# Layer 0 attention: the last 24 modulation columns as TensorE products between the query tiles

## The chip, the cores and the metric

The kernel runs on one core of one Trainium2 chip. Its time is the device time of one execution in microseconds. Three executions of the kernel before took 2327.45, 2328.95 and 2331.25 us, so the median is 2328.95 us. The profile is of one further execution.

The names of the engines here are those of the profile: PE is the matrix engine (TensorE), PEld its weight loads, DVE the vector engine, ACT the scalar engine, POOL GpSimd, and SP the engine that issues most DMAs.

## The reference, cut to what matters

The model has two layers. Layer 0 modulates its normed tokens with shifts, scales and gates that come from a conditioning vector, once for the latent tokens (condition `c`) and once for the context tokens (condition `c_ctx`):

```python
def adaln(cond, w, b):
    return jax.nn.silu(cond) @ w + b

mod_lat = adaln(c, mod_w[i], mod_b[i])[:, None, :]
mod_ctx = adaln(c_ctx, mod_w[i], mod_b[i])[None, None, :]
sh1, sc1, g1, sh2, sc2, g2 = jnp.split(mod_lat, N_MOD, axis=-1)
csh1, csc1, cg1, csh2, csc2, cg2 = jnp.split(mod_ctx, N_MOD, axis=-1)
```

`mod_w[0]` is 1024 x 6144. Cut into blocks of 128 outputs it has 48 blocks, called columns in the kernel, since each gives one column of 128 numbers per condition. Blocks 0 to 15 are `sh1` and `sc1`, 16 to 23 the gate `g1` behind the attention, 24 to 39 `sh2` and `sc2` of the feed-forward, 40 to 47 the gate `g2`. This case is about blocks 16 to 39, both conditions: 24 blocks, 48 results.

The attention of layer 0 has 6 heads. Each has two score matrices, and the second softmax is subtracted from the first, scaled by lambda. There are 512 latent queries with 768 keys, and 256 context queries with 256 keys.

## The kernel before, in words

Products with weights are made in three passes (`mm3`): weights and activations are split into a high and a low part (fp32r), and PE multiplies high by high, high by low and low by high, at lines L108, L109 and L110. A product of plain f32 operands is shown as two PE records for each instruction.

In the attention the work goes by units: a head h (0 to 5) and a query tile u (0 to 5) of 128 queries. For each unit `scores` (L428) makes the two score matrices of the next tile in the PSUM tile `pS`; DVE takes the row maximum (L407) and ACT the exponential (L408). Then `combine` works on the present tile: DVE joins the two softmax matrices (L447), PE transposes the result in blocks of 128 into `ptr` (L452), ACT and DVE split that into high and low (L133), and at every second tile PE multiplies by the values into `prb` (L108 to L110 with `prb`), which ACT copies out (L461). There is one buffer `prb`. Between these parts a generator `fill` gives out the input projection of the next head (L108 to L110 with `pz`), and in heads 0 and 1 the pooling branch.

The columns are fitted in one a unit, from unit 1 on (24 units, so to the first of head 4), by `mod_both`. For each column SP loads a 128 x 1024 block of the transposed weight (L288). DVE multiplies it by the row of condition 0 and sums along the row in one instruction (L292). POOL then multiplies the block by the row of condition 1 in four pieces of 256 (L301), and ACT sums it (L303). The bias is added later for all columns at once (`mod_bias`, L307).

The order on each engine is made by a scheduler that walks the program with its own estimates of times; the program's order and the `behind` hints bound it. Each engine runs its queue strictly in that order, so an instruction that waits holds up all that stand behind it on the same engine. Input weights are loaded into three buffers `w_raw` (L87), which SP issues in one queue with the column loads.

Of the kernel before, what the change touches and what calls it, by code (L numbers as in the profile page):

```python
# [43 lines left out]
def behind(tc, ins):  # L44

    return tc.issue_after(getattr(ins, "ins", ins))
# [16 lines left out]
class Kernel:  # L63
# [228 lines left out]
            nc.vector.scalar_tensor_tensor(self.m_junk, w, 1.0, self.crow[:, cd, :], op0=OP.mult, op1=OP.mult,  # L292
                                           accum_out=self.mods[:, layer, cd, n:n + 1])

    def mod_both(self, n):


        self.mod_dve(0, n, (0,))
        w = self.m_raw[(self.m_next - 1) % len(self.m_raw)]
        for i in range(0, D, 256):  # L300
            self.nc.gpsimd.tensor_mul(w[:, i:i + 256], w[:, i:i + 256], self.crow[:, 1, i:i + 256])  # L301
        yield
        self.nc.scalar.activation(w, w, AF.Copy, accum_out=self.mods[:, 0, 1, n:n + 1])  # L303

    def mod_bias(self, layer, t0, n, cd):
        m = self.mods[:, layer, cd, t0:t0 + n]
# [127 lines left out]
    def combine(self, h, u, sc):  # L434


        nc, wk, wb, sm = self.nc, self.work, self.workb, self.small
        (p0, p1), z, nkt = sc
        if u == 0:
            self.oT = wb.tile([128, TA], F32, name="oT", bufs=2)  # L440
        if u % 2 == 0:
            self.pt = [wb.tile([128, 6, 256], F32R, name=f"pt{x}", bufs=1) for x in "hl"]
        (pth, ptl), oT = self.pt, self.oT
        rz = sm.tile([128, 1], F32, name="rz", bufs=4)
        nc.vector.reciprocal(rz, z[:, 1, u:u + 1])
        nc.vector.tensor_scalar(rz, rz, z[:, 0, u:u + 1], self.nlam, op0=OP.mult, op1=OP.mult)
        ins = nc.vector.scalar_tensor_tensor(p0, p1, rz, p0, op0=OP.mult, op1=OP.add)  # L447
        for k0 in range(0, nkt, 4):
            n = min(4, nkt - k0)
            pt = self.ps.tile([128, 4, 128], F32, name="ptr", bufs=1)  # L450
            for k in range(n):
                nc.tensor.transpose(pt[:, k, :], p0[:, (k0 + k) * 128:(k0 + k + 1) * 128], self.ident)  # L452
            qs = slice(u % 2 * 128, u % 2 * 128 + 128)
            self.split(pth[:, k0:k0 + n, qs], ptl[:, k0:k0 + n, qs], pt[:, :n])
        if u % 2:
            vh, vl = self.heads[h][2]
            kt0 = 6 - nkt
            po = self.ps.tile([128, 512], F32, name="prb", bufs=1)[:, :256]
            self.mm3(po, lambda i: (vh[:, kt0 + i, :], vl[:, kt0 + i, :]),
                     lambda i: (pth[:, i, :], ptl[:, i, :]), n=nkt)  # L460
            nc.scalar.copy(oT[:, u // 2 * 256:u // 2 * 256 + 256], po)  # L461

        if u < 2:
            next(self.head_end, None)
        if u == 5:
            self.head_end = self.norm_head(h, oT, z)
            next(self.head_end)
            if h == 5:
                for _ in self.head_end:
                    pass  # L470
        return ins
# [76 lines left out]
    def layer0_mixer(self):  # L548
        nc, I, tc = self.nc, self.I, self.tc
        self.mix_d = self.dram.tile([KT - 2, 128, TA], F32, name="mix_d")  # L550
        with ExitStack() as ctx:
            a = self.a = self.new_a(LAT, CTX)
            mspace = self.hm.tile([128, KT * TA], F32, name="hm")
            self.m_space = self.mod_space(mspace, 2)
            wk = self.work = self.pool(ctx, "workA")
            c2 = ctx.enter_context(ExitStack())
            xp = self.xp = self.pool(c2, "xp")
# [41 lines left out]
            with behind(tc, self.m_after):  # L599
                nc.sync.dma_start(self.pw, I["pool_w"])  # L600
                nc.sync.dma_start(lmb, I["lam"][None, :, :].to_broadcast([128, 4, 64]))
                self.cond_rows()
            norm(blat, LAT)

            def lam():
# [24 lines left out]
                pass  # L630
            c2 = ctx.enter_context(ExitStack())
            self.workb = self.pool(c2, "workB")
            self.m_raw.append(self.workb.tile([128, D], F32, name="m3", bufs=1))
            self.head_end = iter(())
            todo, sums = list(range(16, 40)), iter(())
            fill = {0: [self.inproj_head(1), self.pool_branch(0)], 1: [self.inproj_head(2), self.pool_branch(1)],
                    2: [self.inproj_head(3)], 3: [self.inproj_head(4)], 4: [self.inproj_head(5)],
                    5: [self.out_latent()]}
# [2 lines left out]
            for i, (h, u) in enumerate(units):  # L641
# [8 lines left out]
                            next(g, None)  # L650
                if u == 5 and h < 5:
                    nxt, pe = self.scores(h + 1, 0)
                with behind(tc, self.exped):
                    next(sums, None)
                if todo and i:
                    with behind(tc, dv):
                        sums = self.mod_both(todo.pop(0))
                        next(sums)
                cur = nxt
            c2.close()  # L660
            for _ in fill[5][0]:
# [8 lines left out]
    def out_latent(self):  # L670

        nc, I, wk, tc = self.nc, self.I, self.work, self.tc
        for cd in range(2):
            self.mod_bias(0, 16, 8, cd)
        self.mix = self.new_a(LAT, CTX)
        for k in range(KT - 1):
            if k == KT - 2:
# [21 lines left out]
    def out_rest(self):  # L699
# [12 lines left out]
        for d in range(KT - 3, KT):  # L712
# [3 lines left out]
                for e in range(KT - 3):  # L716
                    last(e, 0)
            full(d, 0)
        for cd in range(2):
            self.mod_bias(0, 24, 16, cd)  # L720
        self.hm_d = self.dram.tile([128, KT, TA], F32, name="hm_d")
        self.B = {}
        hi, lo = (self.big.tile([128, KT, TL], F32R, name=f"a{x}512").rearrange("p k t -> p (k t)") for x in "hl")
# [1075 lines left out]
def tiles(w, nt=128):  # L1799

    K, N = w.shape
    return np.ascontiguousarray(w.reshape(K // 128, 128, N // nt, nt).transpose(2, 1, 0, 3)).reshape(N // nt, 128, -1)
# [35 lines left out]
def layouts(inp):  # L1838
# [8 lines left out]
    A["gains"] = cols(np.stack([a["norm1_g"][0], a["norm2_g"][0], a["norm1_g"][1], a["norm2_g"][1]]))  # L1847
    A["misc"] = np.concatenate([cols(a["pool_scale"][0]), cols(a["q_norm_g"][0]), cols(a["kv_norm_g"][0])], axis=1)
    A["mod_n"] = tiles(a["mod_w"][0][:, :2048], 512)
    A["mod_t"] = np.ascontiguousarray(a["mod_w"].transpose(0, 2, 1)).reshape(2, 48, 128, D)  # L1850
    w = a["even_w_in"][0]
    order = [w[:, :256]]
# [67 lines left out]
```

## Time and profile before

| what | value |
|---|---|
| median of three runs | 2328.95 us |
| profiled execution, its own time | 2319.6 us |
| its span, first to last instruction | 2317.9 us |
| PE busy over the span | 2251.2 us, 97% |
| DVE busy | 1765.4 us, 76% |
| ACT busy | 1212.2 us, 52% |
| POOL busy | 198.3 us, 9% |
| mean granted clock of PE | 0.989 |

Busy time is the union of an engine's records. PE's records overlap, as one matmul starts before the last has drained, so the time that one really takes is read from start to start. The attention of layer 0 runs from about 85 to 415 us of the span. A granted clock of 1.00 is 2.4 GHz, of 0.50 it is 1.2 GHz.

### The profile page before, as it was taken

What the parts mean: (1) busy time and instruction counts of PE and PEld (TensorE: products, weight loads), DVE (VectorE), ACT (ScalarE), POOL (GpSimd) and SP (SyncE); (2) the same over time, 40 slices, a digit from 0 to 9 for tenths busy, and PEclk for the clock granted to TensorE, in tenths of its full rate; (3) what the DMA queues carried; (4) which work ended last, traced back from release to release, by engine and by line L of the source; (5) the groups of instructions that cost most, each with busy time, mean ns of one, the idle gap of its engine ahead of it and who ended that gap; (6) DMA issues with size and microseconds to landing.
All of it is one profiled execution on the core that took longest, in us unless ns stands there. A gap on an engine that the chain in (4) does not pass through costs nothing.

```text
span 2317.9 us, 31085 instructions
## 1 busy us (share of the span) xinstructions
PE 2251.2 (97%) x11672; PEld 1833.2 (79%) x11672; DVE 1765.4 (76%) x2547; ACT 1212.2 (52%) x1690; POOL 198.3 (9%) x273
## 2 busy tenths in 40 slices
PE   8999998999999999999999899999999999999996
PEld 3777777899999988888888777777777777777774
DVE  4779876687877876477775798787877778777897
ACT  3445553453334432245553676566655666555764
POOL 0033410000000111000000000010000000000030
PEclk9999998999999999999999999999999999999998
DMA  7233322335444596311122797787777877777794
GB/s 295 80 105 106 107 77 95 110 132 165 143 141 152 198 377 240 126 42 42 35 85 78 275 362 293 282 304 274 266 276 275 315 263 288 267 285 272 275 399 175
DMA packets 97505, 467.97 MB, mean 202 GB/s; under 512 B 11232, under 2 KB 13664, under 8 KB 63556
## 3 DMA queue, kind: packets, MB, share of 16 engines
q1 hardware_dynamic: 76000, 386.83, 45.9%
q0 software_dynamic: 19680, 76.90, 9.2%
q10 hardware_dynamic: 1668, 2.18, 0.3%
q8 instruction: 94, 1.54, 0.3%
q14 instruction: 63, 0.52, 0.1%
HBM read 435.19 MB, written 30.68 MB: 201 GB/s over the span
## 4 chain that ended last, share of the span: by engine, by line
PE 85%; DVE 6%; ACT 2%; DMA 1%; issue 1%; POOL 0%; DVEq 0%; ACTq 0%
PE pz L109 11%; PE pz L108 11%; PE pz L110 11%; PE pS L818 10%; PE pS L973 5%; PE pz L818 4%; PE pS L108 4%; PE pS L109 4%; PE pS L110 3%; PE pz L1490 3%; PE pz L1489 3%; PE pz L973 2%; PE prb L108 1%; PE prb L109 1%; PE prb L110 1%; DVE u_lo L133 1%
## 5 line engine op out<-in xcount | busy, mean ns | idle before, releaser
L133 DVE TENSOR_TENSOR u_lo<-u_raw,u_hi 128x2048 fp32r<-128x2048 f32 x264 | 601.8, 2285 | 154.7 <-ACT u_hi L133 154.5
L133 ACT CAST u_hi<-u_raw 128x2048 fp32r<-128x2048 f32 x264 | 502.4, 1909 | 199.5 <-issue 69.6
L109 PE MATMUL pz<-u_lo,x 128*128 128x512 f32 x704 | 283.7, 403 | 6.2 <-DVE u_lo L133 6.0
L108 PE MATMUL pz<-u_hi,x 128*128 128x512 f32 x704 | 282.0, 401 | 0.5 <-ACT u_hi L133 0.5
L110 PE MATMUL pz<-u_hi,x 128*128 128x512 f32 x704 | 279.9, 398 | 0.0
L108 PE MATMUL pz<-ah,w_hi 128*128 128x512 f32 (+1 forms) x513 | 183.4, 358 | 1.1 <-DVE n_tmp L325 0.6
L109 PE MATMUL pz<-al,w_hi 128*128 128x512 f32 (+1 forms) x513 | 178.8, 349 | 0.0
L110 PE MATMUL pz<-ah,w_lo 128*128 128x512 f32 (+1 forms) x513 | 178.2, 348 | 0.0
L109 PEld LDWEIGHTS pz<-u_lo,x 128*128 128x128 f32 x704 | 132.5, 188 | 46.0 <-DVE u_lo L133 18.7
L108 PEld LDWEIGHTS pz<-u_hi,x 128*128 128x128 f32 x704 | 132.4, 188 | 29.9 <-ACT u_hi L133 1.0
L110 PEld LDWEIGHTS pz<-u_hi,x 128*128 128x128 f32 x704 | 132.5, 188 | 28.5
L292 DVE SCALAR_TENSOR_TENSOR n_acc<-ms 128x1024 bf16<-128x1024 f32 x80 | 97.4, 1217 | 19.0 <-DMA ms<-in_mod_t_dram 18.9
L108 PEld LDWEIGHTS pz<-ah,w_hi 128*128 128x128 f32 x513 | 97.3, 190 | 14.9 <-issue 0.9
L97 ACT CAST w_hi<-w_raw 128x1024 fp32r<-128x1024 f32 (+2 forms) x69 | 58.6, 851 | 93.3 <-PE pz L109 63.2
L110 PEld LDWEIGHTS pz<-ah,w_lo 128*128 128x128 f32 x513 | 97.2, 190 | 11.0 <-issue 0.5
L109 PEld LDWEIGHTS pz<-al,w_hi 128*128 128x128 f32 x513 | 97.6, 190 | 10.5 <-issue 0.7
L109 PE MATMUL pS<-u_lo,hs 128*128 128x512 f32 x264 | 105.1, 398 | 0.7 <-DVE u_lo L133 0.7
L1489 PE MATMUL pz<-u_hi,x 128*128 128x512 f32 x264 | 105.3, 399 | 0.0
L108 PE MATMUL pS<-u_hi,hs 128*128 128x512 f32 x264 | 104.6, 396 | 0.5 <-ACT hs L133 0.5
L110 PE MATMUL pS<-u_hi,hs 128*128 128x512 f32 x264 | 104.6, 396 | 0.0
L1490 PE MATMUL pz<-u_lo,x 128*64 128x512 f32 x264 | 98.5, 394 | 0.0
L408 ACT ACTIVATE P<-pS,mx 128x768 f32<-128x768 f32 (+1 forms) x104 | 83.3, 804 | 19.7 <-DVE mx L407 19.4
(561 smaller groups left out, 5431.8 us busy)
## 6 DMA issues: line engine op xcount, KB each, us to landing
u_raw<-in_moe_w_dram SPq DMA_DIRECT2D x264, 1024.0 KB, 4.9
ms<-in_mod_t_dram POOLq DMA_DIRECT2D x56, 512.0 KB, 4.9
hr<-hid_d SPq DMA_DIRECT2D x38, 384.0 KB, 6.0
w_raw<-in_w_gate_dram SPq DMA_DIRECT2D x28, 512.0 KB, 3.5
w_raw<-in_w_in_dram SPq DMA_DIRECT2D x27, 512.0 KB, 3.3
u<-in_w_up_dram SPq DMA_DIRECT2D x22, 512.0 KB, 3.7
w_raw<-in_w_dn_dram SPq DMA_DIRECT2D x22, 512.0 KB, 4.7
hid_d<-hm POOLq DMA_DIRECT2D x22, 384.0 KB, 3.1
```

What stands on the lines that cost most here:

```text
L97: nc.scalar.copy(hi[:, :n], raw[:, :n])
L108: nc.tensor.matmul(ps, wh, xh, start=first and i == 0, stop=False)
L109: nc.tensor.matmul(ps, wh, xl, start=False, stop=False)
L110: ins = nc.tensor.matmul(ps, wl, xh, start=False, stop=last and i == n - 1)
L133: return nc.scalar.copy(hi, src), nc.vector.tensor_sub(lo, src, hi)
L292: nc.vector.scalar_tensor_tensor(self.m_junk, w, 1.0, self.crow[:, cd, :], op0=OP.mult, op1=OP.mult, accum_out=self.mods[:, layer, cd, n:n ...
L408: self.exped = nc.scalar.activation(P, S, AF.Exp, bias=nm, accum_out=z)
L818: nc.tensor.matmul(ps, w[m][:, c], x[n][:, k, :], start=first and k == i == 0, stop=k == 3 and i == 2, skip_group_check=True)
L973: nc.tensor.matmul((pl, px)[cd][d], W[w][:, d * 128:d * 128 + 128], x[v][:, s], start=n == i == 0 and not (cd and d % 2), stop=n == NF - 1 ...
L1489: m = [lambda s, e: self.nc.tensor.matmul(ps, x[2][:, k, :], w(k)[0], start=s, stop=e), lambda s, e: self.nc.tensor.matmul(ps[:64], x[0][: ...
L1490: lambda s, e: self.nc.tensor.matmul(ps[:64], x[0][:, k, :], w(k)[1], start=s, stop=e)]
```

## The change

The 24 columns leave DVE, POOL and ACT and become products on PE. The weight block itself, in its plain layout (`mod_k`, 128 inputs x 128 outputs for each of 8 slices), is the stationary operand, and the two conditions' silu vectors `scol` are two moving columns. One column takes 8 matmuls into two PSUM columns. Two columns (16 matmuls) are done at every second tile, u = 1, 3 and 5, from head 0 to head 3, 12 times in all, ahead of the tile's transposes. The PSUM tile is the one that the product with the values uses later in the same tile (`prb`, its columns 256 to 259); it is taken at the start of `combine` for that. A small DVE addition adds the bias and stores both columns. There are four weight buffers, all loaded ahead by SP, and each is loaded again after its use. The rows of the conditions (`cond_rows`) are no longer loaded here, and the two late additions of the bias are gone.

```diff
-    def mod_both(self, n):
-        self.mod_dve(0, n, (0,))
-        w = self.m_raw[(self.m_next - 1) % len(self.m_raw)]
-        for i in range(0, D, 256):
-            self.nc.gpsimd.tensor_mul(w[:, i:i + 256], w[:, i:i + 256], self.crow[:, 1, i:i + 256])
-        yield
-        self.nc.scalar.activation(w, w, AF.Copy, accum_out=self.mods[:, 0, 1, n:n + 1])
+    def mod_load(self):
+        if self.m_next < 24:
+            self.nc.sync.dma_start(self.m_raw[self.m_next % len(self.m_raw)], self.I["mod_k"][self.m_next])
+            self.m_next += 1
+
+    def mod_cols(self, ps, i0):
+        nc = self.nc
+        for i in range(2):
+            w = self.m_raw[(i0 + i) % len(self.m_raw)]
+            for k in range(KT):
+                nc.tensor.matmul(ps[:, 2 * i:2 * i + 2], w[:, k * 128:k * 128 + 128], self.scol[:, k, :], start=k == 0,
+                                 stop=k == KT - 1, skip_group_check=True)
+            self.mod_load()
+        n = slice(16 + i0, 18 + i0)
+        nc.vector.tensor_add(self.mods[:, 0, :, n], ps.rearrange("p (n c) -> p c n", c=2),
+                             self.modb[:, 0, None, n].to_broadcast([128, 2, 2]))
...
         (p0, p1), z, nkt = sc
+        if u % 2:
+            po = self.ps.tile([128, 512], F32, name="prb", bufs=1)
+            if self.m_todo:
+                self.mod_cols(po[:, 256:260], self.m_todo.pop(0))
+            po = po[:, :256]
...
             kt0 = 6 - nkt
-            po = self.ps.tile([128, 512], F32, name="prb", bufs=1)[:, :256]
             self.mm3(po, lambda i: (vh[:, kt0 + i, :], vl[:, kt0 + i, :]),
...
-                self.cond_rows()
+                for _ in self.m_raw:
+                    self.mod_load()
...
-                with behind(tc, self.exped):
-                    next(sums, None)
-                if todo and i:
-                    with behind(tc, dv):
-                        sums = self.mod_both(todo.pop(0))
-                        next(sums)
                 cur = nxt
...
-        for cd in range(2):
-            self.mod_bias(0, 16, 8, cd)
...
-        for cd in range(2):
-            self.mod_bias(0, 24, 16, cd)
...
+    A["mod_k"] = tiles(a["mod_w"][0][:, 2048:5120])
```

What the scheduler makes of it is seen in the order on the engines. First PE, in head 0 at tile 1, before the change: `pS` are the scores of the next tile, `ptr<-ident,P` the transposes of this one, and `pz` the input projection of head 1.

```order
L428 MATMUL pS<-qk1h,qk0h 128x256 x2
L428 MATMUL pS<-qk1l,qk0h 128x256 x2
L428 MATMUL pS<-qk1h,qk0l 128x256 x2
L452 MATMUL ptr<-ident,P_627 128x128 x4
L108 MATMUL pz<-ah_98,w_hi 128x256
```

The same place in the changed kernel, with line numbers moved (L437 is L428 of before, L466 is L452):

```order
L437 MATMUL pS<-qk1h,qk0h 128x256 x2
L437 MATMUL pS<-qk1l,qk0h 128x256 x2
L437 MATMUL pS<-qk1h,qk0l 128x256 x2
L307 MATMUL prb<-scol,hm 128x2 x16
L466 MATMUL ptr<-ident,P_628 128x128 x4
L108 MATMUL pz<-ah_98,w_hi 128x256
```

One row is new: 16 matmuls of two columns, between the scores of the next tile and the transposes of this one. There are 12 such rows on PE, one for each pair of columns.

The second place is ACT in head 0 at tiles 2 to 4, before the change: `hm,mods<-hm` is the sum of a column (L303), which reads what POOL has multiplied; `w_hi` is the split of the next weights, and `sq` belongs to the pooling branch.

```order
L133 CAST pth<-ptr 128x4x128
L408 ACTIVATE P_874,zs<-pS,mx 128x768
L408 ACTIVATE P_875,zs<-pS,mx 128x768
L303 ACTIVATE hm,mods<-hm 128x1024
L133 CAST pth<-ptr 128x2x128
L408 ACTIVATE P_964,zs<-pS,mx 128x256
L408 ACTIVATE P_965,zs<-pS,mx 128x256
L303 ACTIVATE hm,mods<-hm 128x1024
L133 CAST qk1h<-pz 128x256
L97 CAST w_hi<-w_raw 128x1024
```

The same place on ACT in the changed kernel (L417 is L408 of before, L543 is L530):

```order
L133 CAST pth<-ptr 128x4x128
L417 ACTIVATE P_887,zs<-pS,mx 128x768
L417 ACTIVATE P_888,zs<-pS,mx 128x768
L133 CAST pth<-ptr 128x2x128
L417 ACTIVATE P_970,zs<-pS,mx 128x256
L417 ACTIVATE P_971,zs<-pS,mx 128x256
L97 CAST w_hi<-w_raw 128x1024
L133 CAST qk1h<-pz 128x256
```

Both sums are gone from ACT's queue, and the casts that stood behind them follow the exponentials at once.

## Rows read from the trace of the kernel before

**Rows 1.** The page, part 1: busy time, share of the span, instructions.
```profile
PE 2251.2 (97%) x11672; PEld 1833.2 (79%) x11672; DVE 1765.4 (76%) x2547; ACT 1212.2 (52%) x1690; POOL 198.3 (9%) x273
```

**Rows 2.** Busy us by stretch: PE, PEld, DVE, ACT, POOL; PEclk, DMA share, GB/s.
```profile
100.00:120.00 20.00, 19.56 (x126) 15.52 (x124) 19.75 (x35) 9.67 (x22) 5.13 (x10) 1.00 0.16 54
120.00:140.00 20.00, 17.74 (x110) 14.23 (x112) 14.57 (x31) 10.31 (x22) 11.59 (x15) 1.00 0.36 125
140.00:160.00 20.00, 19.27 (x108) 14.59 (x107) 17.78 (x33) 10.18 (x21) 7.11 (x9) 1.00 0.38 124
160.00:200.00 40.00, 36.12 (x221) 28.46 (x219) 33.17 (x57) 19.11 (x42) 10.71 (x14) 1.00 0.26 87
200.00:250.00 50.00, 48.68 (x313) 39.07 (x311) 43.80 (x87) 29.64 (x66) 24.56 (x29) 1.00 0.33 114
250.00:300.00 50.00, 49.29 (x311) 39.20 (x309) 42.09 (x83) 28.30 (x62) 19.09 (x25) 1.00 0.30 103
300.00:350.00 50.00, 49.35 (x315) 39.64 (x314) 37.67 (x81) 27.92 (x61) 5.54 (x9) 1.00 0.20 68
350.00:400.00 50.00, 44.16 (x230) 34.37 (x230) 30.42 (x67) 19.00 (x45) 3.19 (x6) 0.86 0.28 100
```

**Rows 3.** The chain that ended last, 85 to 350 us, shares by line.
```profile
by line: PE pz L108 11.9%; PE pz L110 11.6%; PE pz L109 11.6%; PE pS L428 6.8%; PE ptr L452 4.8%; DVE w_lo L98 3.3%; issue 3.0%; PE prb L108 3.0%; DVE n_acc L292 2.8%; PE prb L169 2.8%; PE prb L109 2.5%; DVE mx L407 2.4%; PE prb L110 2.1%; 
```

**Rows 4.** Lines L292, L301 and L303: ns min/median/max, first and last start, form.
```profile
L292 DVE SCALAR_TENSOR_TENSOR n_acc<-hm x16: 1206/1218/1760, 93.0 to 294.6; 128x1024 bf16<-128x1024 f32 x16
...
L301 POOL TENSOR_TENSOR hm<-hm x64: 722/737/1723, 94.3 to 298.0; 128x256 f32<-128x256 f32 x64
...
L303 ACT ACTIVATE hm<-hm x16: 1047/1055/1066, 112.5 to 312.7; 128x1024 f32<-128x1024 f32 x16
```

**Rows 5.** PE in order of time, 136.9 to 139 us: start, us, engine, line, operation.
```profile
137.07 0.28 PE L110 MATMUL pz<-ah,w_lo 128*128 128x256 f32 x1
137.38 1.50 PE L169 MATMUL prb<-ones,sq 128*128 128x1 f32 x12
138.74 0.36 PE L108 MATMUL pz<-ah,w_hi 128*128 128x256 f32 x1
138.94 0.28 PE L109 MATMUL pz<-al,w_hi 128*128 128x256 f32 x1
```

**Rows 6.** PE in order of time, 1264.9 to 1268.6 us.
```profile
1265.34 1.06 PE L1240 MATMUL pS<-rwa,hm 128*128 128x8 f32 x8
1266.26 0.48 PE L108 MATMUL pz<-ah,w_hi 128*128 128x512 f32 x1
```

**Rows 7.** ACT and PE in order of time, about 120 us.
```profile
120.45 1.06 ACT L303 ACTIVATE hm<-hm 128x1024 f32<-128x1024 f32 x1 [1.33 <-POOL hm L301]
...
121.38 0.63 PE L452 MATMUL ptr<-ident,P 128*128 128x128 f32 x4 [0.84 <-DVE P L447]
```

**Rows 8.** Line L278, the nearest small addition from PSUM.
```profile
L278 DVE TENSOR_TENSOR mods<-ptr,modb x4: 157/163/167, 21.3 to 48.1; 128x8 f32<-128x8 f32 x4
```

**Rows 9.** Busy time by stretch, with the granted clock, at five places.
```profile
137.20:138.80 1.60, 1.57 (x15) 1.42 (x13) 0.00 (x0) 0.13 (x1) 0.41 (x1) 1.00 0.00 0
...
1279.20:1284.40 5.20, 5.20 (x50) 5.16 (x50) 1.79 (x6) 1.75 (x4) 0.00 (x0) 1.00 0.00 0
...
1284.40:1287.80 3.40, 3.40 (x19) 3.31 (x17) 3.02 (x26) 2.66 (x5) 0.00 (x0) 0.50 0.01 2
...
458.40:461.80 3.40, 3.40 (x12) 3.12 (x10) 3.31 (x5) 2.19 (x3) 1.43 (x2) 0.50 0.50 169
...
48.80:55.60 6.80, 6.80 (x24) 5.83 (x23) 3.02 (x7) 4.60 (x7) 0.11 (x1) 0.50 0.17 59
```

**Rows 10.** PE in order of time, 1277.7 to 1288 us.
```profile
1280.63 0.96 PE L1240 MATMUL pS<-rwa,hm 128*128 128x8 f32 x8
...
1282.98 0.95 PE L169 MATMUL prb<-ones,n_tmp 128*128 128x1 f32 x8
```

**Rows 11.** DMA issues: KB each, median us from issue to landing.
```profile
hm<-in_mod_t_dram SPq DMA_DIRECT2D x16, 512.0 KB, 3.3
```

More of the change, by code (lines that the diff above doesn't have):

```diff
@@ L553, in layer0_mixer @@
             mspace = self.hm.tile([128, KT * TA], F32, name="hm")
-            self.m_space = self.mod_space(mspace, 2)
+            self.m_raw, self.m_next, self.m_todo = [mspace[:, i * D:(i + 1) * D] for i in range(4)], 0, list(range(0, 24, 2))
+            self.m_space = mspace[:, 4 * D:]
             wk = self.work = self.pool(ctx, "workA")
@@ L632, in layer0_mixer @@
             self.workb = self.pool(c2, "workB")
-            self.m_raw.append(self.workb.tile([128, D], F32, name="m3", bufs=1))
             self.head_end = iter(())
-            todo, sums = list(range(16, 40)), iter(())
             fill = {0: [self.inproj_head(1), self.pool_branch(0)], 1: [self.inproj_head(2), self.pool_branch(1)],
```

## The prediction

> **What bounds the kernel now.** I read the page first: PE is busy for 2251.2 us, 97% of the span, DVE as the next engine for 76% [rows 1]. That share is a mean, so I went to the stage by stretches. From 250 to 350 us, which is heads 3 and 4, PE is busy for 49.29 and 49.35 us of each 50. DVE has 42.09 and 37.67 us and ACT about 28 [rows 2]. The reader is to see one more thing there. The stretch 250:300 holds the column work of a whole head, with 19.09 us on POOL; 300:350 holds the rest of it, with 5.54 us. PE gets through 311 matmul records in the one and 315 in the other. So from head 3 on the column work costs next to nothing: DVE, ACT and POOL do it beside a full PE.
>
> Before 200 us it looks different. In 100:120 DVE is busy for 19.75 of 20 us, and in 120:140 and 160:200 PE lacks 2.26 and 3.88 us [rows 2]. One such place is at 120 us. ACT waits 1.33 us for POOL's product of a column, sums it for 1.06 us, and the casts that stand behind it on ACT are late; shortly after, PE waits 0.84 us for DVE's combined softmax [rows 7]. The chain that ended last, from 85 to 350 us, is nevertheless made of PE lines: the column line L292 has 2.8% of the span it covers, and the three lines of the input projection have 35.1% [rows 3].
>
> So the change takes work from engines that mostly have room and gives it to the one that has none.
>
> **What it removes.** 24 instructions of 1.218 us on DVE, 96 of 0.737 us on POOL, 24 of 1.055 us on ACT [rows 4], that is 29.2, 70.8 and 25.3 us, and the two late additions of the bias. What they are worth is only what PE waits for on their account. PE's idle time from 100 to 350 us is 0.44 + 2.26 + 0.73 + 3.88 + 1.32 + 0.71 + 0.65 = 9.99 us [rows 2]. Where the columns cost nothing (250 to 350 us), 1.36 us in 100 remain, which is 3.4 us over 250. I take the difference as what goes: **-6.6 us**. The bounds are nothing and the whole 9.99 us. What is late next in these places is PE itself.
>
> **What it adds on PE.** The trace has no such product, but it has two neighbours: plain f32, a 128x128 stationary block, one or eight moving columns. With one column, twelve records stand between 137.38 and 138.74 us, 0.1133 us each. Entering and leaving such a run costs a little more: 0.31 us from the last projection record instead of the usual 0.12, and 0.20 instead of 0.12 behind the first record after it, 0.27 us together [rows 5]. With eight columns it is 0.92 us for eight records, 0.115 us each [rows 6]. Two columns lie between these. A plain f32 matmul is two records, so a run of 16 matmuls is 32 records: 32 x 0.1133 + 0.27 = 3.90 us, with the other pitch 3.95 us. Twelve runs make **+46.8 us** (46.8 to 47.4). They stand on PE's queue in one piece, ahead of the transposes, and nothing of them can lie beside other PE work. What they can lie beside are PE's waits, and these I have counted above.
>
> **What it does to PE's clock.** This is the term I am least sure of. From 1279.2 to 1284.4 us PE is busy for all of 5.20 us, at a granted 1.00, with matmuls of one and eight columns and 128-column transposes [rows 9, 10]; then the clock is at 0.50 (1.2 GHz) from 1284.4 to 1287.8 us, though the queue never ran empty [rows 9]. A run of twelve one-column records, 1.36 us long, left it at 1.00 [rows 9]. A run of the change is 3.90 us, nearer to the long stretch than to the short one, and of two columns throughout. So I take it that each of the 12 runs brings one stretch at half clock of the length of 458.4 to 461.8 us, 3.4 us [rows 9]. Work that PE does in it takes twice as long, so a stretch loses 1.7 us: **+20.4 us**. The lower bound is nothing, as after the short run; the upper a stretch of 6.8 us a run, as at 48.8 us [rows 9], which is 12 x 3.4 = 40.8 us. I keep both for the range.
>
> The Trainium skill (TensorE: Matmul & The Clock Gate, HAM oscillation — how this bites in real kernels) lays the fall to gaps between bursts of matmuls, in which PE has nothing to run. By that rule the runs, which leave no gap, would keep 2.4 GHz, and the sum would lack the third term. The trace speaks against the rule at 1284.4 us, where there is no gap. [...]
>
> **What costs nothing.** The 12 additions of the bias read PSUM and take about 0.16 us each, as a like one of 128x8 [rows 8]; DVE has lost 29.2 us and has room. The column loads are of the same number and size, 24 of 512 KB, on SP's queue as before, landing after 3.3 us [rows 11]. Each pair waits until PE has read the pair that it replaces, and `w_raw` loads stand behind it on SP; but a pair is used two runs, so four tiles, later, some 30 us at 50 us for the six tiles of a head, and input weights are loaded three ahead. If that cover were gone, a late pair would cost its landing, 3.3 us, ten times at the most. `prb` is claimed ahead of the transposes now, so PE could wait there for its last reader; that is ACT's copy of two tiles before or DVE's product for the head's norm, both done some units earlier, so I take zero.
>
> **The sum.** 46.8 + 20.4 - 6.6 = +60.6 us. Against the profiled execution, 2319.6 us, that is 2380.2 us. The runs shown have their median 9.35 us higher, at 2328.95 us, so I carry the difference over: **2389.6 us**.
>
> **The rivals.**
>
> *The clock holds* (the skill's rule above). For it: the one-column run at 137 us, and that heads 1 to 4 keep 1.00 throughout. Against it: 1284.4 us. It leaves 46.8 - 6.6 = +40.2 us, 2369 us, and with all idle time gone +36.8 us, 2366 us.
>
> *The clock falls for longer.* [...] 46.8 + 40.8 - 6.6 = +81.0 us, 2410 us.
>
> *DVE paces heads 0 to 2.* PE's records overlap, so a busy share of 97% may hide waits, and 19.75 of 20 us on DVE in 100:120 speaks for DVE as the bound there. Then the runs of heads 0 to 2, nine of twelve, lie beside DVE's work and cost nothing, and the time falls by what leaves DVE there, 17 columns of 1.218 us and their reading out, some 22 us. The three runs of head 3 are paid, 11.7 us. Together -10 us, 2319 us: faster. It decides once PE's waits in heads 0 to 2 exceed the nine runs, 35 us. Against it: only 9.99 us of idle time show [rows 2], and removing the columns is worth nothing in the heads that follow.
>
> *The loads are late*, and the runs wait for their weights: +60.6 us and up to 33 us more, 2423 us. Nothing in the SP queue speaks for it.
>
> **How the numbers follow.** The forecast has 0.60, the clock that holds 0.23, the longer fall 0.09, DVE as the bound 0.05, late loads 0.03. A measurement of this kernel can tell about 0.2%, 4.7 us, from no change. Only the DVE case is faster, and a part of it would land within that bound: faster 0.04, within 0.03, slower 0.93. The range reaches down over the clock that holds, with its stronger saving, to 2361 us, and up to 2408 us, which leaves out most of the longer fall and the late loads and the whole of the faster case.
>
> **What would show it.** In the profile after, the new line has 384 records on PE, a start every 0.11 us in runs of 3.6 to 4 us; if the pitch is under 0.05 us, the second term is wrong. The granted clock in 85 to 350 us, 1.00 before, should fall to about 0.93 in that stage (12 x 3.4 us at half in some 320), with stretches at 0.50 next to the runs; if it stays at 1.00, the first rival holds. DVE's busy time should fall by some 29 us and POOL's by about 70 without the stage getting shorter. The attention should end some 60 us later, and the rest of the kernel should be as long as before. If the stage has as long a PE idle time as before, my first term is wrong.

## The result and the profile after

The changed kernel takes 2379.98 us in the median of 5 runs (2376.78 to 2384.98). The kernel before, on the same chip, takes 2330.62 us (2327.45 to 2332.55): a ratio of 1.0217 [1.0201, 1.0233], about 49 us more. Two later comparisons of the same two kernels gave 1.0253 [1.0238, 1.0268] and 1.0235 [1.0218, 1.0252]. The forecast was +60.6 us: the direction and the range hold, and the move came out about 11 us smaller.

Part 1 of the page after, to be held against [rows 1]: busy time, share of the span, instructions.

```profile
PE 2312.7 (97%) x12056; PEld 1897.7 (80%) x12056; DVE 1731.2 (73%) x2507; ACT 1187.6 (50%) x1642; POOL 118.5 (5%) x177
```

PE has 384 instructions and 61.5 us of busy time more. DVE lost 34.2 us, ACT 24.6 and POOL 79.8. PE's 61.5 us are the 58.5 us by which the profiled span is longer (2376.4 us, 2317.9 before) and 3.0 us of idle time less.

The stretches of [rows 2] in the trace after, in the same columns:

```profile
100.00:120.00 20.00, 19.60 (x128) 16.96 (x126) 14.82 (x28) 8.70 (x20) 1.53 (x2) 0.91 0.24 81
120.00:140.00 20.00, 20.00 (x122) 17.19 (x123) 7.96 (x19) 6.11 (x14) 0.55 (x1) 0.91 0.32 105
140.00:160.00 20.00, 19.38 (x130) 15.98 (x131) 13.47 (x32) 8.74 (x18) 0.54 (x1) 1.00 0.29 91
160.00:200.00 40.00, 39.89 (x236) 31.71 (x235) 24.75 (x41) 12.06 (x23) 1.09 (x2) 0.91 0.31 103
200.00:250.00 50.00, 49.52 (x317) 41.43 (x316) 28.05 (x62) 19.14 (x44) 0.54 (x1) 0.90 0.24 78
250.00:300.00 50.00, 49.41 (x309) 43.02 (x308) 26.19 (x61) 15.93 (x36) 0.00 (x0) 0.89 0.20 67
300.00:350.00 50.00, 49.92 (x307) 44.86 (x308) 21.14 (x49) 15.41 (x36) 0.54 (x1) 0.84 0.14 50
350.00:400.00 50.00, 48.84 (x314) 39.01 (x312) 36.87 (x77) 25.64 (x58) 3.21 (x6) 1.00 0.20 68
```

Three things are to be seen. PE's idle time from 100 to 350 us fell from 9.99 us to 2.28 us. DVE, which had 43.80 and 42.09 us in 200:250 and 250:300, has 28.05 and 26.19, and the stage is longer all the same. And the granted clock, 1.00 throughout this part before, is at 0.84 to 0.91 in all rows but 140:160 and the last. The 0.86 that stood in 350:400 before is not gone: its 13.7 us at half clock, from 356.0 us before, stand from 404.6 us now.

The new line in the trace after, with the durations of its records and what they waited for:

```profile
L307 PEld LDWEIGHTS prb<-scol,hm x384: 186/192/338, 96.1 to 342.9; 128*128 128x128 f32 x192
L307 PE MATMUL prb<-scol,hm x384: 165/251/354, 96.1 to 342.9; 128*128 128x2 f32 x192
...
its engine sat idle before it (us, times) until:
  issue: 0.2, 1
  DVE mx L416: 0.2, 1
```

These are 384 records, as counted in the prediction, and next to no idle time ahead of them: no run ever waited for its weights or for `prb`. The column loads land after 3.9 us (3.3 in [rows 11]):

```profile
hm<-in_mod_k_dram SPq DMA_DIRECT2D x24, 512.0 KB, 3.9
```

PE in order of time around the first run (start, us, engine, line, operation), the answer to [rows 5]:

```profile
95.87 0.28 PE L437 MATMUL pS<-qk1h,qk0l 64*128 64x256 f32 x2
96.08 3.73 PE L307 MATMUL prb<-scol,hm 128*128 128x2 f32 x32
99.67 0.63 PE L466 MATMUL ptr<-ident,P 128*128 128x128 f32 x4
100.06 0.36 PE L108 MATMUL pz<-ah,w_hi 128*128 128x256 f32 x1
```

From its first record to the next line's the run takes 3.59 us, that is 0.112 us a record; leaving it costs nothing extra.

The chain that ended last, 85 to 350 us, as in [rows 3]:

```profile
by line: PE prb L307 17.6%; PE pz L108 16.2%; PE pz L109 15.5%; PE pz L110 15.4%; PE pS L437 7.2%; PE ptr L466 6.0%; PE prb L108 2.5%; PE prb L169 2.2%; PE prb L109 2.1%; PE prb L110 2.1%; DVE w_lo L98 1.8%; PE pz L338 1.6%; PE pz L542 1.6%
```

The column line of DVE (2.8% before) has left the chain, and L307 holds 17.6% of 265 us, 46.6 us. The twelve runs, each from its first record to PE's next line, come to 46.3 us; at the 3.56 us of an undisturbed one they would be 42.7.

The granted clock around the first run, and in two later stretches:

```profile
96.08:99.67 3.59, 3.59 (x34) 3.59 (x33) 3.59 (x4) 0.11 (x1) 0.21 (x4) 1.00 0.42 129
99.67:100.80 1.13, 1.13 (x12) 1.13 (x12) 0.30 (x2) 0.46 (x1) 0.00 (x0) 1.00 0.59 203
100.80:104.20 3.40, 3.40 (x18) 3.40 (x18) 1.68 (x2) 1.91 (x5) 0.00 (x0) 0.51 0.67 259
274.90:281.70 6.80, 6.80 (x34) 6.80 (x34) 0.59 (x2) 0.90 (x3) 0.00 (x0) 0.50 0.48 154
322.70:329.50 6.80, 6.80 (x34) 6.80 (x34) 2.20 (x6) 1.88 (x6) 0.00 (x0) 0.50 0.00 0
```

The run itself is at 1.00; the clock falls 1.1 us behind its end, and PE has not been idle for a moment. In heads 0 to 3 there are 11 stretches at 0.50, seven of 3.4 us and four of 6.8 us, 51.2 us in all. Ten of them begin inside a run or within 1.2 us of its end, one begins 11 us behind; two runs (at 136.5 and 170.8 us) are followed by none. The one that begins 11 us behind, at 227.1 us, follows by 1.2 us a run of twelve one-column records, the sums for head 1's norm (L169). The first experiment shows the same fall where no column work is on PE.

### The profile page after: what moved, and what is told of

The parts are those of the page before. It is cut to its first block, busy times and chain, and to the rows that moved or that the text cites. A ratio compares the mean times of both kernels' runs of the same rounds, so it can differ in the third digit from the quotient of the medians.

```text
span 2376.4 us, 31615 instructions
## 1 busy us (share of the span) xinstructions
PE 2312.7 (97%) x12056; PEld 1897.7 (80%) x12056; DVE 1731.2 (73%) x2507; ACT 1187.6 (50%) x1642; POOL 118.5 (5%) x177
## 4 chain that ended last, share of the span: by engine, by line
PE 91%; DVE 4%; DMA 2%; ACT 1%; issue 1%; ACTq 0%; DVEq 0%; SPq 0%
PE pz L109 12%; PE pz L108 12%; PE pz L110 12%; PE pS L821 10%; PE pS L976 5%; PE pz L821 4%; PE pS L108 4%; PE pS L109 4%; PE pS L110 4%; PE pz L1493 3%; PE pz L1492 3%; PE pz L976 2%; PE prb L307 2%; PE prb L108 1%; PE prb L109 1%; PE pS L437 1%
## 5 line engine op out<-in xcount | busy, mean ns | idle before, releaser
L108 PE MATMUL pz<-ah,w_hi 128*128 128x512 f32 (+1 forms) x513 | 189.8, 370 | 0.8 <-DVE n_tmp L334 0.6
L109 PE MATMUL pz<-al,w_hi 128*128 128x512 f32 (+1 forms) x513 | 185.3, 361 | 0.0
L110 PE MATMUL pz<-ah,w_lo 128*128 128x512 f32 (+1 forms) x513 | 183.8, 359 | 0.0
L109 PEld LDWEIGHTS pz<-u_lo,x 128*128 128x128 f32 x704 | 133.2, 189 | 46.1 <-DVE u_lo L133 18.6
L110 PEld LDWEIGHTS pz<-u_hi,x 128*128 128x128 f32 x704 | 133.2, 189 | 28.7
L108 PEld LDWEIGHTS pz<-ah,w_hi 128*128 128x128 f32 x513 | 103.7, 202 | 14.5 <-DVE n_tmp L339 0.8
L292 DVE SCALAR_TENSOR_TENSOR n_acc<-ms 128x1024 bf16<-128x1024 f32 x80 | 97.4, 1217 | 21.5 <-DMA ms<-in_mod_t_dram 21.1
L109 PEld LDWEIGHTS pz<-al,w_hi 128*128 128x128 f32 x513 | 103.4, 202 | 11.0 <-issue 1.0
L110 PEld LDWEIGHTS pz<-ah,w_lo 128*128 128x128 f32 x513 | 102.9, 201 | 11.1 <-issue 0.2
L416 DVE TENSOR_REDUCE mx<-pS 128x1 f32<-128x768 f32 (+1 forms) x104 | 84.3, 827 | 11.1 <-PE pS L1140 6.8
```

What stands on the lines that cost most here:

```text
L108: nc.tensor.matmul(ps, wh, xh, start=first and i == 0, stop=False)
L109: nc.tensor.matmul(ps, wh, xl, start=False, stop=False)
L110: ins = nc.tensor.matmul(ps, wl, xh, start=False, stop=last and i == n - 1)
L416: nc.vector.reduce_max(nm, S, axis=AX.X, negate=True)
```

## The experiments

All are compared by one measure, taken from the PE records of each profiled execution: the time from the first score product (L437 here, L428 before) to the first record of the sums for a head's norm (L169), for heads 0 to 3, in which the changed kernel has its columns, and for each head. "Half" is the time in heads 0 to 3 at 0.50, "idle" PE's idle time there, "to head 5" the stage up to head 5's norm.

```
kernel        heads 0, 1, 2, 3, 4, 5 (us)            0 to 3   half  idle  to head 5
before        61.2 72.0 40.8 49.1 49.4 65.0          223.1    0.0   9.8   337.5
changed       67.7 80.8 58.1 65.3 49.4 65.9          271.9   51.2   2.7   387.2
after_again   69.0 85.4 58.1 65.3 49.4 65.8          277.8   64.9   2.6   393.0
after_third   69.0 85.3 58.1 65.3 49.4 65.6          277.7   64.9   2.6   392.7
x1_no_cols    58.5 68.2 42.7 48.9 49.2 64.2          218.2    3.4   5.7   331.6
x2_split      66.4 83.8 57.0 59.8 51.4 65.3          267.1   34.6   1.4   383.8
x6_spread     64.7 78.2 51.8 60.5 49.9 65.0          255.3    6.8   2.7   370.2
x11_quarters  66.6 82.1 50.1 63.8 49.8 64.5          262.6   20.5   3.0   376.9
x8_one        59.3 75.7 47.8 54.9 49.4 64.8          237.7   17.1   2.4   351.9
x3_late       58.5 69.9 40.8 49.1 54.4 69.1          218.3    0.0   6.0   341.8
x4_dve_both   61.0 67.6 47.7 51.8 48.2 63.5          228.1    6.8   6.4   339.7
x10_mix       61.0 69.3 43.4 49.1 49.4 63.5          222.7    6.8   5.1   335.6
```

Two things bear on how rows compare. In the kernels with columns on PE, 24 records of the input projection stand ahead of the first score product that stand behind it in the others, where they take 3.1 us of the measure:

```profile
76.16 0.50 PE L428 MATMUL pS<-qk1h,qk0h 64*128 64x512 f32 x2
76.62 0.38 PE L108 MATMUL pz<-ah,w_hi 128*128 128x256 f32 x1
...
79.48 0.28 PE L110 MATMUL pz<-ah,w_lo 128*128 128x256 f32 x1
79.69 0.50 PE L428 MATMUL pS<-qk1l,qk0h 64*128 64x512 f32 x2
```

And the clock's last fall can reach past head 3's norm: x2_split's, of 6.8 us, counts here with 0.5 us, and x6_spread and x11_quarters have one of 3.4 us that begins 1.4 and 1.1 us behind that norm.

The whole loss lies in heads 0 to 3: the attention is 49.7 us longer up to head 5's norm, heads 0 to 3 are 48.8 us longer, and heads 4 and 5 differ by 0.9 us. What follows the attention took 1913.3 us in the changed kernel's profile, and 1910.2 to 1916.1 us in those of the seven other runs with the same routing behind it, among them three versions of the kernel before. The profile of before has 1904.3 us there: that one execution was short, which is why the two spans differ by 58.5 us and the medians by 49.

**No columns at all (x1_no_cols).** The columns are left out and read as zero, so the attention keeps its work but the routing after it is another one; only the stage can be compared.

```diff
+        nc.vector.memset(self.mods[:, 0, :, 16:40], 0.0)
...
-            if self.m_todo:
-                self.mod_cols(po[:, 256:260], self.m_todo.pop(0))
...
-                for _ in self.m_raw:
-                    self.mod_load()
```

> The changed kernel without the 24 columns: their loads, products and additions are left out, and the columns are zero instead (so the tokens are routed to the experts differently, and only the attention stage, from the first score product to the last transposes of the softmax, is compared; it is 332.4 us in the kernel before and 382.2 us in the changed one). It shows alone what it is worth to take the columns off DVE, POOL and ACT. As forecast, where only PE's visible idle time goes: 6.6 us, a stage of 326 us. If PE also lost time under its overlapping records, as the sum of the changed kernel's trace (46.3 us of runs, some 21 us of half clock beside them, +49.8 us) suggests: some 18 us, a stage of 314 us. If DVE paced heads 0 to 2: over 22 us, a stage under 310 us.

In the expectation's measure, up to the last transposes, the stage takes 326.6 us against 332.4: its first case. Heads 0 to 3 take 218.2 us, with 3.4 us at half clock; at full clock about 216.9. Against 223.1 us before, this prices the columns where they were: 6.2 us, all that another place for them can win there. They cost it in heads 0 and 1, 126.7 us here and 133.2 before; heads 2 and 3 are no shorter, 91.6 us with the 3.4 us at half clock, 89.9 before. Its stretches show what remains:

```profile
100.00:120.00 20.00, 19.41 (x120) 14.61 (x118) 19.62 (x38) 10.53 (x23) 1.53 (x2) 1.00 0.14 48
120.00:140.00 20.00, 19.33 (x122) 16.08 (x121) 10.25 (x28) 8.73 (x20) 1.09 (x2) 1.00 0.32 93
...
160.00:200.00 40.00, 37.77 (x229) 28.75 (x227) 32.52 (x58) 18.54 (x42) 1.09 (x2) 1.00 0.17 60
```

PE's wait of 2.26 us in 120:140 [rows 2] is 0.67 here. In 160:200 it still waits 2.23 us without any column work; in the changed kernel 0.11 us of that is left.

The 3.4 us at half clock come here without any column work, 1.6 us behind the one-column records of head 1's norm:

```profile
200.52 1.50 PE L169 MATMUL prb<-ones,hm 128*128 128x1 f32 x12 [0.39 <-ACT hm L489]
201.95 0.39 PE L438 MATMUL pS<-qk1l,qk0h 64*128 64x256 f32 x2
```

```profile
203.60:207.00 3.40, 3.40 (x11) 2.62 (x10) 2.30 (x9) 1.84 (x5) 0.00 (x0) 0.51 0.01 2
```

So not every fall in the table belongs to the new records. In nine of the twelve profiles the clock falls within that run of head 1 or up to 1.7 us behind it; before, x3_late and x11_quarters have no fall there.

**Half a run at a time (x2_split).** One tile's eight matmuls ahead of the transposes, the other's behind the product with V.

```diff
-            if self.m_todo:
-                self.mod_cols(po[:, 256:260], self.m_todo.pop(0))
...
+            pm, i0 = po[:, 256:260], self.m_todo.pop(0) if self.m_todo else None
+            if i0 is not None:
+                self.mod_cols(pm, i0, 0)
...
+            if i0 is not None:
+                self.mod_cols(pm, i0, 1)
```

> The changed kernel with each run of 16 matmuls in two: the first column ahead of the tile's transposes, the second behind its product with the values. Same work, runs of 1.8 us. If the clock falls for the length of the runs, it stays at 1.00 in the attention and the time falls by what the half clock cost: 20.4 us by the forecast's term, 21 to 25 us by the stretches in the changed kernel's trace, so 2355 to 2360 us. If the half clock cost little (the rival: 10 us, with a saving of only 6.6 us elsewhere), 2370 us. If half runs pull it down as well, 2380 us with the same stretches at 0.50.

2377.38 us, 1.021 [1.0191, 1.0229]: not to be told from the changed kernel's first comparison (1.0217), and below its two later ones. Runs of half the length leave 34.6 us at half clock where the changed kernel had 51.2; heads 0 to 3 are 4.8 us shorter. So the clock fell behind runs of 1.8 us too.

**Quarter runs, one at every query tile (x6_spread, x11_quarters).** In x6_spread the four matmuls of a piece go ahead of and behind other products in the same bank of PSUM without being sums of their own, so the columns come out different and with them the routing behind the attention; only the stage is compared. (The 41.0 us that the expectation gives for x2_split are its 34.6 us and the part of its last fall in head 4.)

```diff
+        w = self.m_raw[n % len(self.m_raw)]
+        for k in range(k0, k1):
+            nc.tensor.matmul(ps, w[:, k * 128:k * 128 + 128], self.scol[:, k, :], start=k == 0,
+                             stop=k == KT - 1, skip_group_check=True)
...
+            here = c is not None and u % 2 == 0 and k0 + 4 >= nkt
+            if here:
+                self.mod_part(pt[:, 3, :2], c, 0, 4)
...
+            if here:
+                self.mod_part(pt[:, 3, :2], c, 4, KT)
```

> The changed kernel with its 192 matmuls spread further: one column in each of 24 tiles (units 0 to 23), each column in two pieces of 4 matmuls (0.9 us), in even tiles in the free columns of the transposes' PSUM tile. Same work on PE, 42.7 us. Settles what the half clock costs the changed kernel, since half runs did not lift it (heads 0 to 3: 271.9 us with 51.2 us of half clock in the changed kernel, 267.0 us with 41.0 us in the half runs, 218.3 us with 3.4 us and without any columns). If a stretch costs half its length on the whole, as in the forecast, and the runs partly lie beside waits of PE: with the clock at 1.00, heads 0 to 3 take 248 to 252 us and the kernel 1.2% more than before. If the runs are paid in full and the half clock costs only some 11 us: 259 to 262 us, 1.7% more than before. If the clock still falls: 265 to 272 us.

The same 384 records, but only 6.8 us at half clock, and heads 0 to 3 take 255.3 us, 16.6 us less than in the changed kernel and between the expectation's first two cases. PE's records and its idle time (2.7 us) are as many there, so the difference goes to the clock; the count in the next part bears this out. One of the two falls, at 222.1 us, lies in the one-column run of head 1's norm. x11_quarters does the same with pieces that are sums of their own, for the price of another addition on DVE for each tile, so that its whole time can be read too.

```diff
-            nc.tensor.matmul(ps, w[:, k * 128:k * 128 + 128], self.scol[:, k, :], start=k == 0,
-                             stop=k == KT - 1, skip_group_check=True)
+            nc.tensor.matmul(ps, w[:, k * 128:k * 128 + 128], self.scol[:, k, :], start=k == k0,
+                             stop=k == k1 - 1, skip_group_check=True)
+        m = self.mods[:, 0, :, 16 + n:17 + n]
+        b = m if k0 else self.modb[:, 0, None, 16 + n:17 + n].to_broadcast([128, 2, 1])
+        nc.vector.tensor_add(m, ps.rearrange("p (n c) -> p c n", c=2), b)
```

> All 24 tiles of columns on TensorE, each in two pieces of four matmuls that are sums of their own in two places of PSUM, one piece at a time at every query tile, and two additions on DVE for each tile. Theory (the work on PE costs about 36 us net of waits, and the rest of the change's cost is half clock that comes with runs of 3.6 us): half clock in heads 0 to 3 stays under 15 us, heads 0 to 3 last 250 to 260 us, ratio to before 1.012 to 1.017. Rival (the clock falls with any such work, and the spread run before had its 6.8 us by luck): 35 us or more at half clock, heads 0 to 3 at 266 us or more, ratio 1.019 or more. Second rival (48 more additions on DVE take back what leaves it): little half clock, but heads 0 to 3 over 262 us with PE idle for over 8 us.

20.5 us at half clock and 262.6 us for heads 0 to 3, between what the theory and the first rival gave; the second rival falls, PE is idle for 3.0 us. The time is 2371.68 us, 1.0205 [1.0181, 1.0228] beside a before of 2325.92 us; that ratio is where the first rival had it. The changed kernel beside it on the same chip (after_third) took 2383.03 us, 11 us more in the median, but one of the five runs here (2382.64) lies among its runs. The stage accounts for 39.4 of the 45.8 us, and the attention's start, with the 24 records, for 1.9 more; the rest lies within the spread of its runs (2369.34 to 2382.64). One of its falls, with PE in order of time and then the clock around it:

```profile
206.47 1.05 PE L306 MATMUL prb<-scol,hm 128*128 128x2 f32 x8
207.46 0.38 PE L437 MATMUL pS<-qk1h,qk0l 64*128 64x256 f32 x2
207.77 1.05 PE L306 MATMUL ptr<-scol,hm 128*128 128x2 f32 x8
208.69 0.55 PE L108 MATMUL pz<-ah,w_hi 128*128 128x256 f32 x1
```

```profile
137.00:208.70 71.70, 70.00 (x453) 57.87 (x451) 42.88 (x89) 25.19 (x51) 1.64 (x3) 1.00 0.24 77
208.70:215.50 6.80, 6.80 (x34) 6.80 (x34) 1.57 (x7) 1.04 (x5) 0.00 (x0) 0.50 0.43 145
215.50:294.00 78.50, 77.66 (x530) 64.39 (x529) 46.99 (x117) 30.76 (x66) 0.54 (x1) 1.00 0.23 80
```

Two pieces stand close together here, and the clock falls as the second ends. In three other places, at 131.2 (with one transpose record between them), 263.6 and 325.8 us, two pieces have come together into one run of 16 records (1.8 us); behind the first and the third it falls too, 0.6 us after their end. The fourth fall, at 294.0 us, comes after 20 records in three parts since 289.6 us, as the next piece begins. In between it stays at 1.00 for 70 us and more. The distance of two pieces does not decide it alone, though: in x6_spread pieces stand 0.3 us apart in 12 places, and only one of its two falls comes within 3 us behind such a pair. What holds over all runs is the order: pieces of 8 records 6.8 and 20.5 us, runs of 16 records 34.6 us (24 of them; 17.1 us with the 12 of x8_one), runs of 32 records 51.2 to 64.9 us at half clock. What settles a single fall stays open.

**Half the columns (x8_one).** Each run has only its first tile's eight matmuls; the second tile's columns are copies of the first's, and again only the stage is compared.

```diff
-            for k in range(KT):
+            for k in range(KT if i == 0 else 0):
```

> The changed kernel with only the first column of each run (8 matmuls, 12 runs of 1.8 us); its result is also written in place of the second column, so 12 columns are wrong, the routing to the experts differs, and only the attention is compared. Half the work of the change on PE, 21.4 us. If runs of 1.8 us that are two tiles apart leave the clock alone and are paid in full: heads 0 to 3 take 218.3 + 21.4 = 240 us. If they partly lie beside PE's waits: 230 to 235 us. If the clock falls here too: over 240 us, with stretches at 0.50.

Heads 0 to 3 take 237.7 us with 17.1 us at half clock. This comes from one execution. With the half clock taken off (6.3 us, at 0.37 us each as below) it is 231.4 us, 14.5 more than without columns, for 12 x 1.78 = 21.4 us of records (half of 3.56 a run). Of the 6.9 us that do not show, 3.1 are the projection records that stand ahead of the measure; the rest fits PE's idle time, 5.7 us without columns and 2.4 here.

**The old columns, begun later (x3_late).** The kernel before, with its column work starting at query tile 8 of 36 in place of 1.

```diff
-                if todo and i:
+                if todo and i >= 8:
```

> The kernel before, with its columns on DVE, POOL and ACT, but from unit 8 (head 1, tile 2) to 31 instead of 1 to 24. If the columns cost PE some 18 us in heads 0 to 2 and next to nothing behind them, a third of the heads' columns moves out of the bad place: 5 to 9 us faster than before, 2322 to 2326 us. If only the visible idle time of 6.6 us was theirs: 2 to 3 us faster, 2328 us. If they cost the same everywhere, or the late ones collide with the mixed tokens' loads in head 5: not faster.

2333.28 us, 1.0027 [1.0012, 1.0043]. Heads 0 to 3 take 218.3 us, 4.8 less, and heads 2 and 3 are to 0.1 us as long as before though they hold the columns: these cost only in heads 0 and 1. But eight columns now stand in heads 4 and 5 (one before), and these heads lose 9.1 us:

```profile
340.00:347.70 7.70, 2.98 (x26) 2.74 (x25) 3.28 (x4) 3.18 (x7) 2.49 (x3) 1.00 0.48 180
347.70:368.20 20.50, 15.27 (x61) 10.87 (x61) 16.53 (x40) 11.24 (x25) 4.45 (x6) 0.50 0.28 96
```

PE is idle for 4.72 of 7.70 us before the clock falls, for 20.5 us. This is the other way for it to fall in this kernel: with PE waiting. The kernel before has it too, from 356.0 us, for 13.7 us. Which of the loads and queues there makes PE wait was not taken apart.

**Both conditions on DVE (x4_dve_both), and for eleven tiles only (x10_mix).** The kernel before, with both products of a column on DVE and none on POOL and ACT; in x10_mix for tiles 16 to 26, the later ones as before.

```diff
-        self.mod_dve(0, n, (0,))
+        self.mod_dve(0, n, (0, 1))
...
-        for i in range(0, D, 256):
-            self.nc.gpsimd.tensor_mul(w[:, i:i + 256], w[:, i:i + 256], self.crow[:, 1, i:i + 256])
...
-        self.nc.scalar.activation(w, w, AF.Copy, accum_out=self.mods[:, 0, 1, n:n + 1])
```

> The kernel before with both conditions' sums on DVE (two instructions of 1.22 us a column), nothing of the columns on POOL and ACT. Tells which engine's part cost PE its time. If ACT's wait for POOL was it (1.33 us at 120 us, with the casts behind it): faster than before, by up to 18 us, 2313 us. If DVE's load was it: slower, by about what DVE gains in heads 0 to 2, 17 columns of 1.3 us, 2352 us. If neither, 2331 us.

> A version that may beat both. The kernel before, but the 11 columns of heads 0 and 1 (units 1 to 11) have both conditions' sums on DVE and nothing on POOL and ACT, as the run with both on DVE had throughout; the other 13 columns stay as before. That run was 4.6 us shorter than before in heads 0 and 1 (128.6 against 133.2 us) and 9.6 us longer in heads 2 and 3. If ACT's waits for POOL are what the columns cost in heads 0 and 1, and DVE's load what they cost later: some 4.6 us faster than before, a ratio of 0.998. If the order that the scheduler makes of it decides instead: no difference, or slower by a few us.

x4_dve_both: 2334.51 us, 1.0041 [1.0027, 1.0055]. Heads 0 and 1 are 4.6 us shorter, without the wait of ACT for POOL [rows 7], though DVE has more to do; heads 2 and 3 are 9.6 us longer. By the count of the next part, 3.2 of the 9.6 us are the clock's, 1.8 are 15 records that stood in the neighbouring heads before, and 4.6 are waits of PE. That DVE's load makes these waits is not shown; DVE is busy for 88 to 90% here, and was for 83 to 88% before [rows 2]:

```profile
160.00:200.00 40.00, 38.30 (x239) 30.40 (x238) 35.33 (x65) 16.97 (x38) 1.09 (x2) 1.00 0.29 97
200.00:250.00 50.00, 48.11 (x285) 38.01 (x283) 45.01 (x98) 21.19 (x48) 0.54 (x1) 0.97 0.31 101
250.00:300.00 50.00, 48.76 (x287) 37.94 (x288) 43.88 (x92) 21.23 (x48) 0.54 (x1) 0.97 0.29 97
```

x10_mix takes the gain in heads 0 and 1 (2.9 us) and avoids most of the loss, and comes to 2325.8 us, 0.9998 [0.9987, 1.0009]: no difference. No version that ran beats the kernel before.

**The changed kernel again (after_again, after_third).** No edit.

> The changed kernel a second time, unaltered, beside the others on the same chip: how far its stretches at half clock and the length of heads 0 to 3 (271.9 us in its first profile, with 51.2 us at half clock) repeat from one execution to another. If the clock's fall hangs on the runs, 40 to 60 us of heads 0 to 3 at 0.50 again, and 268 to 275 us.

> The changed kernel once more, beside the quarter pieces, to see how far its half clock varies from one profiled execution to the next. Theory: 50 to 65 us at half clock in heads 0 to 3, which last 271 to 279 us; ratio to before 1.020 to 1.026. Rival (the half clock is an accident of two profiles): under 35 us, and heads 0 to 3 under 266 us with the same ratio.

2384.18 us, 1.0253 [1.0238, 1.0268], and 2383.03 us, 1.0235 [1.0218, 1.0252]. Both profiles have 64.9 us at half clock in heads 0 to 3, 13.7 us more than the first, and are 5.9 us longer there (277.8 and 277.7 us). That is above what was expected of after_again, and within what was expected of after_third. The half clock is no accident, and how much of it an execution gets is part of the kernel's spread.

## Why the prediction was right, step by step

The terms can be parted by a count of PE's records in heads 0 to 3. Each record is taken from its start to the start of the next, and its price is the median of its form (output tile and shape) at full clock over the twelve profiles. What a record takes beyond its price at full clock is waiting of PE, shown as idle time or hidden under the overlap of records. What it takes beyond it at 0.50 is put down to the clock.

```
kernel        prices   beyond, at 1.00   beyond, at 0.50   heads 0 to 3 (us)
before        203.6         19.5               0.0              223.1
x1_no_cols    203.6         13.1               1.6              218.2
changed       243.5          3.0              25.4              271.9
x6_spread     243.6          8.4               3.2              255.3
```

```
                              predicted   measured   worked out as
waits that go with the columns   -6.6       -6.4     13.1 - 19.5
runs on PE                      +46.8      +43.0     384 records at their price
records ahead of the measure       -        -3.1     243.5 - 203.6 - 43.0
other waits of PE that go          -       -10.1     3.0 - 13.1
PE's clock                      +20.4      +25.4     (+30 in the two later profiles)
sum                             +60.6      +48.8     271.9 - 223.1
```

These are estimates: with the lower quartile as price in place of the median, the five terms are -6.6, 42.6, -3.1, -12.3 and 28.2. The records ahead of the measure are not saved; they lengthen what stands before the attention.

**What it removes** was right in size, in part by luck. The forecast took PE's visible idle time, less that of an undisturbed stretch, for what the columns cost. Without columns that idle time falls by 4.1 us only (9.8 to 5.7 in heads 0 to 3). The other 2.3 of the 6.4 us were waits hidden under overlapping records, and more than half of the idle time has other causes.

**What it adds** had the right mechanism and the wrong size. The pitch is 0.112 us, as estimated from [rows 5]. But "leaving such a run" costs nothing: the 0.27 us taken for the two ends make 3.2 us in 12 runs, and with the pitch the records come to 42.7 us in place of 46.8. The step that failed is the sentence that the runs "can lie beside PE's waits, and these I have counted above": I had counted only those that vanish with the columns. Waits of other origin, 13.1 us without columns, are 3.0 us in the changed kernel. In x6_spread, with the same records and little half clock, they are 8.4 us, so some 4.7 us go beside the records themselves and some 5.4 us with the slow stretches.

**The clock** was right in kind and too small. I took 12 stretches of 3.4 us, 40.8 us, each costing half its length. There are 51.2 to 64.9 us, since some stretches are 6.8 us long. In its own records, by the median price, a microsecond at half clock costs PE 0.46 to 0.50 us in the seven profiles with columns on PE, so half was nearly right. In the length of the stage it costs less. The six profiles with all 384 records lie within 1.3 us of the line 253.8 us + 0.37 x the time at half clock, and between two executions of the changed kernel it is 0.43, since PE's other waits are the shorter the more of its time is at half clock: by the count 7.5 to 9.5 us in x2_split, x6_spread and x11_quarters, and 3.0 to 4.2 us in the three profiles of the changed kernel. A run of records at half clock takes nearly twice as long, 0.213 us a record against 0.112.

The clock's term was 5 us too small and the waits' 10 us: the two misses have opposite signs, and that the sum came within 12 us owes something to luck.

**What costs nothing** held: L307 waited 0.4 us in all, loads and `prb` included.

**The rivals.** The clock that holds has fallen: 51.2 us at 0.50 with PE idle for 2.7 of 271.9 us, so by the rule of the Trainium skill that was weighed (TensorE: Matmul & The Clock Gate, HAM oscillation — how this bites in real kernels) this stage would have kept its clock, and the trace does not agree. x6_spread comes near to what that rival would have brought: 255.3 us with 6.8 us at half clock, 32.2 us more than before; the rival's price was 40.2 us, without the waits of other origin. The longer fall came true for four of eleven stretches, and for six of thirteen in the later profiles, but 51.2 to 64.9 us at half clock are not the 81.6 us (12 x 6.8) of its price. DVE as the bound of heads 0 to 2 has fallen: without any columns these heads gain 4.6 us (174.0 to 169.4, with 3.4 us at half clock in it), not 22, and with the runs they lose 32.6 us. Its premise was half right: PE's waits were 19.5 us by the count, twice the idle time that shows, but most of them were not the columns'. Late loads did not occur.

## What to carry to other kernels

Work moved from engines that have room to the engine that has none costs its full length there (43.0 us here), less only the waits that this engine still has, those of other origin included. The busy share of the giving engines says little about what is won (6.4 us here); the taker's idle time in the same stretch says it better, though waits can hide under overlapping records and some have other causes. Long runs of matmuls with two moving columns cost a second time, in the clock of what follows; if such work has to be on TensorE, short pieces with wide products between them cost the least in the stage (16.6 us less in x6_spread and 9.3 in x11_quarters than with runs four times as long). Whether the whole time is shorter by as much is not clear of the spread of the runs.

## What the runs showed of the hardware

- The granted clock fell with no idle time on PE, behind runs of 32 records with two moving columns (3.59 us) and of 16 records (about 1.8 us). With 48 pieces of 8 records it fell twice in heads 0 to 3 of x6_spread and four times in x11_quarters, where some pieces had come together.
- It also fell behind the twelve one-column records of a head's norm, with no column work on PE and 0.4 us of idle time ahead of them (x1_no_cols at 203.6 us, x4_dve_both at 207.6, x10_mix at 206.4); other such runs left it at 1.00 [rows 9].
- A plain f32 matmul with 128x128 weights takes 0.112 us a record with two moving columns, with one (0.113, [rows 5]) and nearly so with eight (0.115, [rows 6]), and 0.213 us at half clock. The weight load of such a record is 192 ns in the median, and PE and PEld are both busy throughout the run.
- A microsecond at half clock cost PE 0.46 to 0.50 us in its own records, and this stage, in which PE is busy for 99%, 0.37 to 0.43 us.
